# Last two thirds of the modulation: from TensorE row sums to GpSimd products with one-column matmuls

## The chip, the cores and the metric

The kernel runs on one core of one Trainium2 chip. The metric is device time in microseconds (us) of one execution; the median of three runs counts. Times in a profile are those of one profiled execution.

## The reference, cut to what matters

One transformer block over 1024 tokens of width 1024. A condition vector `c` is turned into six vectors of 1024 numbers, the modulation:

```python
c_act = silu(c)
mod = c_act @ w_ada + b_ada            # 1024 x 6144 weights, one row of c
sh1, sc1, g1, sh2, sc2, g2 = split(mod, 6)
h = rmsnorm(x, norm_attn_g) * (1 + sc1) + sh1
proj = h @ w_in                        # q, k, v of two kinds of attention, gate z, b, a
y = concat(dilated_attention(...), gated_deltanet(...)) @ w_out
x = x + g1 * y
h = rmsnorm(x, norm_ffn_g) * (1 + sc2) + sh2
x = x + g2 * ((silu(h @ w_gate) * (h @ w_up)) @ w_down)
return rmsnorm(x, final_norm_g)
```

`sh1` and `sc1` are needed at once. `g1`, `sh2`, `sc2`, `g2` (columns 2048 to 6143 of `w_ada`, the last two thirds) are needed only after the attention, for the first time where the output projection is added to `x`.

## The kernel before, in words

All arithmetic is in fp32. Large matmuls are made of three products of split operands: a weight tile `wr` is loaded, ScalarE rounds it to `wh` (line 215, or 328 for the first projection), and GpSimd writes the remainder `wl = wr - wh` (line 216, or 329). So nearly every projection matmul waits for a product of GpSimd.

The stages, in the order of the program:

1. Small tables, then the first projection (banks `f0` to `f5`, lines 223 to 395): for each of eight slices of `x`, SyncE's queue loads `xt` (line 246) and `wf` (line 249); ScalarE and GpSimd split `wf`; ScalarE scales `x` into `hh` (line 342).
2. `delta(0)` and `delta(1)`, the gated delta rule in two groups of four heads: convolutions, transposes, decay masks `dt` (loaded by line 685, cut to a triangle on GpSimd by line 692), matrices `kk` (line 776), their storing to DRAM in pieces (`lt_d`, line 789), an inverse that is a serial chain on VectorE (lines 862 and 866, begun with the load of `nt` on line 846), and a scan over eight chunks.
3. While those run, TensorE gets filling work from a generator `others()`: gate projections `z0` (eight blocks `g_z0_0` to `g_z0_7`, line 590), then `kd`, `qd`, `vd`, `z1`, `va` and the attention's q and k. Each `z0` block is read out of PSUM by ScalarE (line 611) into one of two buffers `zt`, multiplied by GpSimd (line 612) and stored (line 617); the buffer is free again when the store has landed.
4. Attention, output projection, and the feed-forward part, which fills the second half of the span.

The modulation's last two thirds are a generator as well, `modulation()`. `mixed()` takes one step of it whenever `others()` has handed out more than `MODS` microseconds of filling. There are 64 steps: eight groups `i` of 512 columns, times eight row blocks `k` of 128 rows. A step loads one block `wm` of 128 x 512 (256 KB) into a buffer shared with other tiles (tag `tc`, three buffers), and `rows4` (line 190) multiplies it on TensorE: the condition's column is the stationary operand, 32 columns wide (one of them used), the block is the moving one, in four strips, so that the sums of 512 columns stand on four partitions of a PSUM bank `mods`. After eight steps VectorE transposes the row into columns (`by_columns`).

The order of instructions on every engine and queue is fixed when the program is built. A scheduler takes instructions by priority as soon as their operands and buffers are free in its own account; `urgent()` raises the priority of what stands inside it by 6000 places, and the loads of the `wm` blocks stand inside it. On the chip each engine, and SyncE's one DMA queue, then goes through its list strictly in order and waits where a semaphore isn't there yet.

Of the kernel before, what the change touches and what calls it, by code (L numbers as in the profile page):

```python
# [10 lines left out]
F32 = mybir.dt.float32  # L11
F32R = mybir.dt.float32r
AF = mybir.ActivationFunctionType
ALU = mybir.AluOpType
# [4 lines left out]
P = 128  # L19
T = 1024  # L20
D = 1024
KT = D // P
TB = T // P
HALF = 512
# [1 line left out]
NF = FT // 2  # L26
SKEW = 4
TCB = 3
MODS = 1.9
EARLY = 1  # L30
LEVELS = ("qd", 4), ("z1", 28)
TAIL = 4
# [37 lines left out]
def build(tc, I, out):  # L70
    nc = tc.nc
    es = ExitStack()
    op = es.enter_context

    def pool(name, side="left", bufs=1, space=None):
        st = ExitStack()
        kw = {} if space is None else {"space": space}
        p = st.enter_context(
            tc.tile_pool(name=name, bufs=bufs, side=side, reuse_waits="tile", **kw)
        )  # L80
        return p, st
# [7 lines left out]
    def const(shape, name, dt=F32):  # L89
        return cp.tile(shape, dt, name=name, tag=name)  # L90

    def urgent():
        return tc.high_priority(offset=6000)
# [8 lines left out]
    ones = onesr.bitcast(F32)  # L102
    nc.gpsimd.affine_select(
        out=tri, in_=tri, pattern=[[1, P]], compare_op=ALU.is_ge, fill=0.0,
# [9 lines left out]
    def small(name, shape, src):  # L114
        t = const(shape, name)
        nc.sync.dma_start(t, src)
        return t


    pd, sd = pool("pd")  # L120
    wp, swp = pool("wp", side="right")
    pv, spv = pool("pv", side="right")
# [7 lines left out]
    def psb(name, tag, bufs):  # L130
        return pg.tile([P, HALF], F32, name=name, tag=tag, bufs=bufs)

    def gbank(name):
        return psb(name, "g", 2)
# [4 lines left out]
    def tbank(name):  # L139
        return psb(name, "t", 2)  # L140

    def abank(name):
        return psb(name, "a", 1)

    def ybank(name):
        return psb(name, "y", 1)

    def start(name, tag, shape=None, dt=F32):

        n = {"xp": 2, "qk": 4, "lu": 5, "o": 2, "VN": 2, "R": 1, "tc": TCB, "yt": 1, "os": 1, "zl": 1}.get(tag, 2)  # L150
        return pd.tile(shape or [P, T], dt, name=name, tag=tag, bufs=n)
# [3 lines left out]
    cc = const([P, KT + 31], "cc")  # L155
# [13 lines left out]
    bada = small("bada", [P, 48], I["bada"])  # L169
    ga = small("ga", [P, KT], I["ga"])  # L170
    mod = const([P, 48], "mod")
# [4 lines left out]
    for j in range(3):  # L176
        n = min(HALF, 1152 - HALF * j)
        ps = tbank(f"ps_R{j}")
# [11 lines left out]
    def rows4(ps, win, w, nt, last):  # L190

        v = w.rearrange("p (t j m) -> p j t m", j=4, m=32)
        for j in range(4):
            nc.tensor.matmul(
                ps[32 * j : 32 * j + 32, 0 : 32 * nt], win, v[:, j], start=False, stop=last, skip_group_check=True
            )

    def by_columns(ps, out, nt, add=None, shape=None, tag="os"):  # L200

        t = shape or start("turned", tag, [P, 256])
        nc.vector.transpose(t[:, 0 : 32 * nt], ps[:, 0 : 32 * nt])
        if add is None:
            nc.vector.tensor_copy(out, t[:, 0 : 32 * nt : 32])
        else:
            nc.vector.tensor_tensor(out=out, in0=t[:, 0 : 32 * nt : 32], in1=add, op=ALU.add)
# [116 lines left out]
    for k in range(KT):  # L324
# [6 lines left out]
        if k == 0:  # L331
            for i in range(KT):
# [4 lines left out]
                out=G1[:, 0:1], in0=mod[:, 8:9], scalar=1.0, in1=ga[:, 0:1], op0=ALU.add, op1=ALU.mult  # L337
            )
            scaled(0, 1)
        for hf in range(2):  # L340
# [3 lines left out]
                out=hl[k][:, cs], in0=xts[k][:, cs], scalar=G1[:, k : k + 1], in1=hh[k][:, cs].bitcast(F32),  # L344
                op0=ALU.mult, op1=ALU.subtract,
# [69 lines left out]
    for i in range(2):  # L415
        ps = aux[:, P * i : P * i + P]
# [183 lines left out]
    for q in range(2):  # L600
        ps = gbank(f"g_qd{q}")
# [30 lines left out]
    def v4(t):  # L632
        return t.rearrange("p (g n h) -> p g n h", g=2, n=8)
# [5 lines left out]
    for g in range(2):  # L639
        nc.vector.tensor_tensor(  # L640
            out=v4(t1)[:, g], in0=ba[:, 1, g], in1=dtb[:, 4 * g : 4 * g + 4].unsqueeze(1).to_broadcast([P, 8, 4]), op=ALU.add
# [437 lines left out]


    def modulation():
        pm = ybank("mods")
        for i in range(8):
            t0 = 16 + 4 * i
            ps = pm[:, P * (i % 4) : P * (i % 4 + 1)]
            if i % 4 == 0:
                nc.vector.memset(pm, 0.0)
            for k in range(KT):
                w = pd.tile([P, HALF], F32, name=f"wm_{i}_{k}", tag="tc", bufs=TCB)
                with urgent():  # L1090
                    nc.sync.dma_start(w, I["wada"][k * P : (k + 1) * P, t0 * P : t0 * P + HALF])
                rows4(ps, cc[:, k : k + 32], w, 4, k == KT - 1)
                yield
            t = pv.tile([P, 256], F32, name=f"mt{i}", tag="zt", bufs=2)
            by_columns(ps, mod[:, t0 : t0 + 4], 4, bada[:, t0 : t0 + 4], shape=t)
        nc.vector.scalar_tensor_tensor(
            out=G2, in0=mod[:, 32:40], scalar=1.0, in1=gff, op0=ALU.add, op1=ALU.mult
        )

    done = set()  # L1100
    mods = modulation()

    def others():
# [19 lines left out]
    def mixed():  # L1123

        t = 0.0
        for c in others():
            yield c
            t += c
            if t > MODS and not quiet[0]:
                t = 0.0  # L1130
# [239 lines left out]
    ps = abank("g2t")  # L1370
# [47 lines left out]
    for hf in range(2):  # L1418
# [3 lines left out]
        for d in range(KT):  # L1422
            slabs = [(wsplit(I["wo"][d, 0], 512, f"wo{d}_0_{hf}"), 0)]
            t = x2[d, hf]
            nc.sync.dma_start(t, _.xp[2 * d + hf])
            ps = (gbank, sbank)[d % 2](f"wo{d}_0_{hf}")
            run(gemm(ps, slabs, yh, yl, cs))
            with urgent():
                nc.vector.scalar_tensor_tensor(
                    out=t, in0=ps, scalar=mod[:, 16 + d : 17 + d], in1=t, op0=ALU.mult, op1=ALU.add,  # L1430
# [14 lines left out]
        ps, pb = ybank(f"ssq2_{hf}"), abank(f"rsb2_{hf}")  # L1445
# [3 lines left out]
        with urgent():  # L1449
            for tb in range(4):  # L1450
# [4 lines left out]
                out=dg, in0=ident.unsqueeze(1).to_broadcast([P, 4, P]),  # L1455
                in1=r4.unsqueeze(2).to_broadcast([P, 4, P]), op=ALU.mult,
# [189 lines left out]
    for k in range(4):  # L1646
# [3 lines left out]
        t = px.tile([P, HALF], F32, name=f"t2_{k}", tag="m", bufs=5)  # L1650
# [231 lines left out]
```

## Time and profile before

| | us |
|---|---|
| runs | 1458.61 median of 3 (1457.56 to 1468.36) |
| span of the profiled execution | 1472.9 |
| TensorE busy | 1400.0 (95%) |
| VectorE busy | 872.2 (59%) |
| ScalarE busy | 667.2 (45%) |
| GpSimd busy | 287.0 (19%), 267 instructions |
| DMA | 244.64 MB, mean 166 GB/s |

In the profile PE is TensorE, PEld its weight load, DVE VectorE, ACT ScalarE, POOL GpSimd, SP SyncE, and SPq SyncE's queue of DMA issues. A row of the timeline reads: start, duration, engine, line, operation, output<-inputs with their shapes, count, and in brackets the idle time before it and what ended it. The page has no other time of the profiled execution than its span, which is 14.3 us above the median of the runs.

### The profile page before, as it was taken

Reading aid. Unit: us, or ns where it says so; the run is one execution under the profiler, and the core shown is the slowest. Engines: PE = TensorE matmul, PEld = TensorE weight load, DVE = VectorE, ACT = ScalarE, POOL = GpSimd, SP = SyncE. Lnnn points to the kernel's source line nnn. Section 1 sums busy time; section 2 is a strip of 40 time slices with the busy share of each in tenths; the row PEclk is TensorE's granted clock in tenths of the full one; section 3 lists DMA queues with packets and bytes.
Section 4 is the critical chain, followed back from the end, with each engine's and each line's share of the span. In section 5 each row is a group of like instructions: output and inputs, shape, how many; then the busy total and the mean of one; then the engine's idle time right before and its main releaser. Section 6 shows DMA issues by size and latency. Waiting matters only on the chain.

```text
span 1472.9 us, 24559 instructions
## 1 busy us (share of the span) xinstructions
PE 1400.0 (95%) x8984; PEld 1140.2 (77%) x8984; DVE 872.2 (59%) x1676; ACT 667.2 (45%) x1279; POOL 287.0 (19%) x267
## 2 busy tenths in 40 slices
PE   7998999988999989999999979999999999999997
PEld 4777767877889868777777758888888888888886
DVE  3687843565733332276525896766666676565477
ACT  3488414248122244476526733333333333445446
POOL 1344512244302332544235000000000000000000
PEclk9998999899957999999999989999999999999999
DMA  8736573475511535743165534454444565866666
GB/s 306 247 108 173 151 221 113 134 218 147 170 46 44 154 104 142 203 129 116 51 220 187 158 122 142 164 160 161 152 157 152 158 217 178 277 206 209 196 219 236
DMA packets 171345, 244.64 MB, mean 166 GB/s; under 512 B 33014, under 2 KB 76327, under 8 KB 171224
## 3 DMA queue, kind: packets, MB, share of 16 engines
q1 hardware_dynamic: 171224, 243.07, 52.7%
q8 instruction: 71, 1.16, 0.3%
q14 instruction: 50, 0.41, 0.1%
HBM read 180.25 MB, written 67.48 MB: 168 GB/s over the span
## 4 chain that ended last, share of the span: by engine, by line
PE 62%; DVE 7%; DMA 5%; ACT 2%; issue 2%; POOL 1%; SPq 0%; ACTq 0%; DVEq 0%
PE wga L1513 8%; PE wua L1513 8%; PE X L1699 6%; PE g_a L567 5%; PE wuc L1513 4%; PE wgc L1513 4%; PE Z L1699 4%; PE wo L567 4%; PE y L1293 3%; PE tr L1276 2%; PE Y L1699 2%; PE g_va L590 2%; PE wub L1513 2%; PE wgb L1513 2%; PE S L1252 1%
## 5 line engine op out<-in xcount | busy, mean ns | idle before, releaser
L1503 DVE TENSOR_TENSOR wl_db<-wr_db,wh_db 128x512 fp32r<-128x512 f32 x77 | 53.2, 691 | 76.1 <-ACT wh_db L1502 75.7
L1502 ACT CAST wh_db<-wr_db 128x512 fp32r<-128x512 f32 x77 | 47.9, 622 | 98.3 <-PE X L1699 41.3
L1699 PE MATMUL X<-wl_db,wh_da 128*128 128x512 f32 x176 | 68.6, 390 | 0.1
L1699 PE MATMUL X<-wh_db,wl_da 128*128 128x512 f32 x176 | 68.5, 389 | 0.0
L1699 PE MATMUL X<-wh_db,wh_da 128*128 128x512 f32 x176 | 68.5, 389 | 0.0
L1263 POOL TENSOR_SCALAR X<-X,sc 128x128 f32<-128x128 f32 (+7 forms) x64 | 47.7, 750 | 67.7 <-DVE sc L1262 55.1
L1261 ACT ACTIVATE X<-X,sc 128x128 f32<-128x128 f32 (+7 forms) x64 | 49.5, 775 | 23.8 <-DVE sc L1256 18.1
L1256 DVE CUSTOM_DVE_ANT_0 X<-S,ng 128x512 f32<-128x512 f32 (+3 forms) x64 | 36.8, 586 | 33.8 <-PE S L1253 21.7
L1222 DVE SCALAR_TENSOR_TENSOR QS<-raw,QS 64x1024 fp32r<-64x1024 f32 x8 | 12.6, 1572 | 70.3 <-ACT QS L1221 70.3
L567 PE MATMUL wo<-yh,wh_wo 128*128 128x512 f32 x128 | 52.0, 408 | 2.1 <-DVE xo L1339 1.0
L1503 DVE TENSOR_TENSOR wl_da<-wr_da,wh_da 128x512 fp32r<-128x512 f32 x77 | 52.6, 685 | 1.2 <-ACT wh_da L1502 1.2
L567 PE MATMUL g_a<-hh,wh_a 128*128 128x512 f32 x128 | 50.6, 395 | 0.0
L567 PE MATMUL g_a<-hh,wl_a 128*128 128x512 f32 x128 | 50.5, 395 | 0.0
L567 PE MATMUL wo<-yh,wl_wo 128*128 128x512 f32 x128 | 50.5, 396 | 0.0
L567 PE MATMUL g_a<-hl,wh_a 128*128 128x512 f32 x128 | 50.2, 392 | 0.0
L567 PE MATMUL wo<-yl,wh_wo 128*128 128x512 f32 x128 | 50.2, 394 | 0.0
L1502 ACT CAST wh_da<-wr_da 128x512 fp32r<-128x512 f32 x77 | 47.3, 616 | 5.8 <-PE wua L1513 5.8
L1293 PE MATMUL y<-et,va 128*64 128x128 f32 x576 | 46.0, 280 | 1.8 <-ACT et L1281 1.8
L1502 ACT CAST wh_wg_s<-wg_s 128x512 fp32r<-128x512 f32 x33 | 20.5, 622 | 58.0 <-PE wuc L1513 22.6
L1276 PE MATMUL tr<-ident,X 128*128 128x128 f32 x288 | 44.5, 280 | 2.2 <-ACT et L1281 2.0
L216 POOL TENSOR_TENSOR wl_wo<-wr_wo,wh_wo 128x512 fp32r<-128x512 f32 x24 | 32.8, 1366 | 57.4 <-ACT wh_wo L215 50.7
L1293 PEld LDWEIGHTS y<-et,va 128*64 128x64 f32 x576 | 33.7, 136 | 12.8 <-issue 8.7
(530 smaller groups left out, 4429.8 us busy)
## 6 DMA issues: line engine op xcount, KB each, us to landing
wr_da<-ao_d SPq DMA_DIRECT2D x77, 256.0 KB, 2.9
wm<-in_wada SPq DMA_DIRECT2D x64, 256.0 KB, 3.5
wr_wg<-in_wg SPq DMA_DIRECT2D x48, 256.0 KB, 3.0
wr_wu<-in_wu SPq DMA_DIRECT2D x48, 256.0 KB, 2.7
ao_d<-a SPq DMA_DIRECT2D x44, 256.0 KB, 2.2
wr_wd<-in_wdn SPq DMA_DIRECT2D x44, 256.0 KB, 3.1
wr_db<-wt_d SPq DMA_DIRECT2D x44, 256.0 KB, 2.7
ao_d<-as SPq DMA_DIRECT2D x33, 256.0 KB, 2.0
```

Of the source, the lines that this page charges most:

```text
L216: (eng or nc.gpsimd).tensor_tensor(out=lo[:, :n], in0=raw[:, :n], in1=hi[:, :n].bitcast(F32), op=ALU.subtract)
L567: last[0] = nc.tensor.matmul(ps, a[:, w0], b[k0 + k4][:, cs], start=(i == 0), stop=(i == n - 1))
L590: last[0] = nc.tensor.matmul(ps[:, :n], a[k][:, ts_], b[:, w0], start=(i == 0), stop=(i == 23))
L1256: nc.vector.tensor_tensor_reduce(out=X[:, c0:c1], in0=ps[:, 0 : c1 - c0], in1=ng[:, u + c0 : u + c1], scale=1.0, scalar=(3e38 if m is None ...
L1261: nc.scalar.activation(X[:, 0:nk], X[:, 0:nk], AF.Exp, scale=-1.0, bias=m, accum_out=sc[:, 2:3])
L1263: nc.gpsimd.tensor_scalar(out=X[:, 0:nk], in0=X[:, 0:nk], scalar1=sc[:, 3:4], scalar2=0.0, op0=ALU.mult, op1=ALU.add)
L1276: nc.tensor.transpose(ps[:, (kb - c0) * P : (kb - c0 + 1) * P], X[:, kb * P : kb * P + P], ident)
L1293: nc.tensor.matmul(yps[64 * e : 64 * e + 64, yc], va[:, kb, 64 * e : 64 * e + 64], ets[e][:, kb, :], start=(kb == 0), stop=(kb == qb),)
L1502: nc.scalar.copy(hi, src)
L1503: (eng or nc.vector).tensor_tensor(out=lo, in0=src, in1=hi.bitcast(F32), op=ALU.subtract)
L1513: nc.tensor.matmul(ps, a[:, w0], b, start=(first and k == 0 and n_ == 0), stop=(k == 3 and n_ == 2), skip_group_check=True,)
L1699: nc.tensor.matmul(bank[b], a[:, ts_], w, start=(first and f == 0 and n_ == 0), stop=(f == NF - 1 and n_ == 2), skip_group_check=True,)
```

## The change

A step of `modulation()` no longer uses TensorE. GpSimd multiplies the block by the condition's column (one number for each partition) and adds it to an accumulator `wa` of 128 x 512; the first block of a group writes the accumulator directly. That is 64 products and 56 sums. When a group's eight blocks are summed, four matmuls with the accumulator's 128 x 128 pieces as stationary operand and a single column of ones as the moving one sum the partitions; their results are columns at once, so the transposes go, and one addition of the bias serves all eight groups. The `wm` blocks get five buffers of their own (tag `wm`), the accumulators two, the loads are asked for three steps ahead, and `MODS` rises from 1.9 to 2.5. The room comes from a smaller scratch area for DMA descriptors.

```diff
-MODS = 1.9
+MODS = 2.5
...
     def modulation():
         pm = ybank("mods")
-        for i in range(8):
-            t0 = 16 + 4 * i
-            ps = pm[:, P * (i % 4) : P * (i % 4 + 1)]
-            if i % 4 == 0:
-                nc.vector.memset(pm, 0.0)
-            for k in range(KT):
-                w = pd.tile([P, HALF], F32, name=f"wm_{i}_{k}", tag="tc", bufs=TCB)
-                with urgent():
-                    nc.sync.dma_start(w, I["wada"][k * P : (k + 1) * P, t0 * P : t0 * P + HALF])
-                rows4(ps, cc[:, k : k + 32], w, 4, k == KT - 1)
-                yield
-            t = pv.tile([P, 256], F32, name=f"mt{i}", tag="zt", bufs=2)
-            by_columns(ps, mod[:, t0 : t0 + 4], 4, bada[:, t0 : t0 + 4], shape=t)
+        units = [(i, k) for i in range(8) for k in range(KT)]
+        ws_, accs = {}, {}
+
+        def load(u):
+            i, k = units[u]
+            ws_[u] = pd.tile([P, HALF], F32, name=f"wm_{i}_{k}", tag="wm", bufs=5)
+            with urgent():
+                nc.sync.dma_start(ws_[u], I["wada"][k * P : (k + 1) * P, (16 + 4 * i) * P : (20 + 4 * i) * P])
+
+        def columns(i):
+            for j in range(4):
+                nc.tensor.matmul(
+                    pm[:, 4 * i + j : 4 * i + j + 1], accs[i][:, j * P : (j + 1) * P], ones[:, 0:1], start=True, stop=True
+                )
+
+        for u in range(3):
+            load(u)
+        for u, (i, k) in enumerate(units):
+            if u + 3 < len(units):
+                load(u + 3)
+            w = ws_.pop(u)
+            if k == 0:
+                accs[i] = pd.tile([P, HALF], F32, name=f"wa_{i}", tag="wa", bufs=2)
+            o = accs[i] if k == 0 else w
+            nc.gpsimd.tensor_scalar(
+                out=o, in0=w, scalar1=cc[:, k : k + 1], scalar2=0.0, op0=ALU.mult, op1=ALU.add
+            )
+            if k > 0:
+                nc.gpsimd.tensor_tensor(out=accs[i], in0=accs[i], in1=w, op=ALU.add)
+            if k == 3 and i > 0:
+                columns(i - 1)
+            yield
+        columns(7)
+        nc.vector.tensor_tensor(out=mod[:, 16:48], in0=pm[:, 0:32], in1=bada[:, 16:48], op=ALU.add)
...
-    nc = _bacc.Bacc("TRN2", target_bir_lowering=False, num_devices=1)
+    nc = _bacc.Bacc("TRN2", target_bir_lowering=False, num_devices=1, dynamic_dma_scratch_size=256)
```

The list of instructions that the build makes of this differs from the list before in three places that the prediction uses. Numbers are places in a queue.

```
SyncE queue, after: places 1-5 the first five wm blocks, 6-10 cc and the tables, 11-31 sixteen more wm blocks
                    (up to group 2, block 4) with bada, ga and the three R_d stores, 32 xt0, 33 wf0
             before: places 1-8 wa8, cc, tables, bada, ga; 9 xt0, 10 wf0
GpSimd, after: places 16-50 the first 20 products and 14 sums, 53 wl_f0;  80-83 the four dt selects of delta(0);
               84-178 the other 44 products and 42 sums, with kt0, kt1, qd0, qd1, zt0_2, U0_0, tt0, zt0_3 among them;
               179 zt0_4, 180 zt0_5, 181 zt0_6, 182 wl_kd2_1
TensorE, after: row 525 columns of groups 0 and 1 (behind g_z0_3), then kk; 583 g_z0_4; 611 columns of group 2, 613 of 3,
                619 of 4, 621 of 5, 623 of 6; 625 g_z0_5, 649 g_z0_6, 673 g_z0_7; 697 g_kd2_0
```

## The prediction

> **What bounds the kernel now.** I read the page first, then TensorE's waits, then the modulation's matmuls by stage, and last the timeline of the start and of the stage in which the modulation runs.
>
> ```profile
> PE 1400.0 (95%) x8984; PEld 1140.2 (77%) x8984; DVE 872.2 (59%) x1676; ACT 667.2 (45%) x1279; POOL 287.0 (19%) x267
> PE   7998999988999989999999979999999999999997
> POOL 1344512244302332544235000000000000000000
> PE 62%; DVE 7%; DMA 5%; ACT 2%; issue 2%; POOL 1%; SPq 0%; ACTq 0%; DVEq 0%
> ```
>
> TensorE is the bound: busy 95%, and no slice but the first, one in the middle and the last is under 80%. GpSimd has much room on average (19%), but all of it is spent in the first 22 slices (810 us), and there it makes the operands that TensorE waits for. So the change takes work from the bound and gives it to an engine with room; what decides is when GpSimd does it. In the profiled execution the span is 1472.9 us, 14.3 above the runs' median of 1458.61; I make the sum as a difference and add it to the median. A measurement of this kernel can tell about 1% (15 us) from no change.
>
> **What TensorE gets back.** The old matmuls by stage (window, then PE busy and instructions), the price of one step among other matmuls, and the waits that they carried:
>
> ```profile
> 165.00:240.00 75.00, 10.80 (x200) 3.98 (x200) 1.43 (x4) 0.98 0.66 197
> 240.00:400.00 160.00, 16.68 (x240) 6.01 (x240) 0.92 (x3) 0.95 0.52 155
> 178.04 0.39 PE L567 MATMUL g_kd<-hl,wh_kd 128*128 128x512 f32 x1
> 178.27 0.39 PE L567 MATMUL g_kd<-hh,wl_kd 128*128 128x512 f32 x1
> 178.59 0.42 PE L196 MATMUL mods<-wm,cc 128*32 128x128 f32 x8
> 178.94 0.50 PE L567 MATMUL g_kd<-hh,wh_kd 128*128 128x512 f32 x1
> 179.28 0.39 PE L567 MATMUL g_kd<-hl,wh_kd 128*128 128x512 f32 x1
> PE mods L196 <- DVE mt L203: 4.3, 2, 3.9
> PE mods L196 <- DMA wm<-in_wada: 4.7, 3, 1.8
> ```
>
> A matmul follows another after 0.23 us (178.04 to 178.27). Around a step it takes 0.67 from 178.27 to 178.94 and 0.34 to 179.28, 1.01 for what would take 0.46: a step of eight records costs 0.55. After 165 us there are 440 records, 55 steps, one of them before the first `kd` matmul at 167.29 (shown below): 54 x 0.55 = 29.7, and one wait of 3.9, together 33.6. The ten steps before 167 I count below, with the stall that swallows them.
>
> The new columns, four matmuls a group, have a near row:
>
> ```profile
> L1451 PEld LDWEIGHTS ssq<-onesr,acc x16: 186/192/192, 787.2 to 817.8; 128*128 128x128 f32 x16
> ```
>
> This is the same form (sum of partitions by a column of ones), 16 records for 8 matmuls, each bound by a weight load of 0.192. A group's four matmuls cost 8 x 0.192 = 1.5 us. All groups but the last stand before the `kd` matmuls, where TensorE will be waiting anyway; the last costs its 1.5. Net 32.1 to gain. The stage is 95% TensorE, but chains of VectorE and ScalarE run beneath it, which the old steps covered in part; I take 80% of it, -26, and keep 0 and -33.6 as bounds.
>
> **What a step costs on GpSimd.** The same forms, fp32, 128 x 512, and what else stands in its queue there:
>
> ```profile
> L1263 POOL TENSOR_SCALAR X<-X,sc 128x512 f32<-128x512 f32 x8 | 5.5, 695 | 9.2 <-DVE sc L1262 7.2 <-PE S L1253 1.2 <-PE tr L1276 0.8
> L1441 POOL TENSOR_TENSOR acc<-acc,sq 128x512 f32<-128x512 f32 x10 | 13.7, 1368 | 9.7 <-ACT sq L1440 9.4
> L1441 POOL TENSOR_TENSOR acc<-acc,sq x10: 1285/1300/1657, 771.0 to 812.7; 128x512 f32<-128x512 f32 x10
> L801 POOL TENSOR_TENSOR kt<-kt,kds 128x1024 f32<-128x1024 f32 x4 | 7.6, 1914 | 9.6 <-ACT kt L722 6.1 <-DVE kds L755 3.5
> L816 POOL TENSOR_TENSOR qd<-qd,eb 128x1024 f32<-128x1024 f32 x4 | 9.5, 2386 | 6.9 <-ACT eb L815 5.3 <-DMA zg_d<-zt 1.6
> L612 POOL TENSOR_TENSOR zt<-zt,ngh 128x256 f32<-128x256 f32 x16 | 14.2, 887 | 38.9 <-ACT zt L611 32.3 <-DMA lt_d<-dt 6.5
> wm<-in_wada SPq DMA_DIRECT2D x64, 256.0 KB, 3.5
> zg_d<-zt SPq DMA_DIRECT2D x16, 128.0 KB, 2.3
> ```
>
> A product 0.695, a sum 1.368 in the mean: 2.06 us a step, 64 x 0.695 + 56 x 1.368 = 121 us in all. Bounds by the sum's least and greatest duration: 1.98 and 2.35. A block takes 3.5 from issue to landing; with five buffers four other steps, 8.2 us, lie between the freeing of a buffer and the use of its next block, so the loads hide. Without that cover each step would be 3.5 longer.
>
> The Trainium skill (GPSIMD Engine Reference, section 4.1, Engine selection) speaks against the change: elementwise sums belong on VectorE, GpSimd is about half as fast with two inputs. Its section 3.1 gives some 2.6 cycles an element for such a sum; at its 1.2 GHz, 512 elements make 1.11 us as an estimate from that page. With that in place of 1.368 the result below would be some 13 us less; the measured row decides.
>
> **The start.** The row blocks are loaded with raised priority, and with five buffers of their own nothing holds them back; so in the written order 21 of them stand ahead of `xt0` in SyncE's queue (place 32), and 34 products and sums ahead of `wl_f0` in GpSimd's. The queue waits at each block for a buffer that GpSimd must free.
>
> ```profile
> 1.40 0.33 SPq L157 DMA_DIRECT2D cc<-in_cc  x1
> 4.39 0.43 SPq L246 DMA_DIRECT2D xt<-in_xT  x1
> 8.94 2.36 SPq L184 DMA_DIRECT2D R_d<-Rs  x3
> 3.86 1.28 ACT L158 ACT_TABLE_LOAD   x1 [3.86 <-DMA cc<-in_cc]
> 5.15 0.21 ACT L158 ACTIVATE cc<-cc 128x8 f32<-128x8 f32 x1
> 11.58 1.27 POOL L329 TENSOR_TENSOR wl_f<-wf,wh_f 128x512 fp32r<-128x512 f32 x1 [9.12 <-ACT wh_f L328]
> 12.18 0.79 PE L236 MATMUL f<-hh,wh_f 128*128 128x512 f32 x1 [0.36 <-ACT hh L342]
> 12.91 0.80 PE L236 MATMUL f<-hh,wl_f 128*128 128x512 f32 x1
> ```
>
> GpSimd can begin when `cc` is through the silu: 5.4 us before; five block issues of 0.4 now stand ahead of it, and their 1.25 MB, so about 8.0. The block before `xt0` needs the buffer of block 16: 16 products and 14 sums, 11.1 + 19.2, and a memset of 0.3, 30.6 us, to 38.6. Its issue and two `R_d` stores take some 1.6: `xt0` is issued at 40.2 instead of 4.39, 35.8 later. Before, the first matmul came 7.8 after that issue and the remainder 8.5, with `wa8` and the stores in between; with those done ahead I take 2.5 off: **+33**. TensorE has nothing else to do: all that follows needs `x`.
>
> **The stall in the middle.** GpSimd's next steps, places 84 to 178, come in one run behind the last `dt` select, and TensorE's own list has the columns of groups 2 to 6 between `g_z0_4` and `g_z0_5`: it stops there until GpSimd has summed group 6.
>
> ```profile
> 131.91 1.09 POOL L692 TENSOR_SCALAR_AFFINE_SELECT dt<-dt 128x1024 f32<-128x1024 f32 x1 [1.36 <-DMA dt<-G_d]
> 164.59 0.28 PE L590 MATMUL g_z<-wh_z,hh 128*128 128x256 f32 x1
> 164.71 0.28 PE L590 MATMUL g_z<-wh_z,hl 128*128 128x256 f32 x1
> 167.17 0.28 PE L590 MATMUL g_z<-wl_z,hh 128*128 128x256 f32 x1
> 167.29 0.40 PE L567 MATMUL g_kd<-hh,wh_kd 128*128 128x512 f32 x1
> ```
>
> The selects end at 133.0, with the start's +33 at 166.0. Up to place 165 follow 39 products and 37 sums, 27.1 + 50.6, two `kt`, two `qd` and a `zt`, 3.8 + 4.8 + 0.9: 87.2, to 253.2. That place frees the buffer of the last block, and in SyncE's queue the store of `zt0_1` stands behind that block's load. `zt` has two buffers, so ScalarE can't read out `g_z0_3` before this store lands, and `g_z0_5` needs its bank: three issues 1.1, landing 2.3, read-out 0.4, to 257.0. Blocks 5 to 7 of `z0` are 72 matmuls at 0.12, 8.7; `g_z0_7` waits besides for `zt0_3` (place 176: 5 products, 4 sums, a memset and itself, 10.9, to 264.1), its store and a read-out, to 267.2, and ends 2.9 later. The first `kd` matmul comes at 270.1 instead of 167.3: 102.8 later, of which the start has 33: **+70**. The steps saved before 167 lie inside this. VectorE's inverse is held as long (its load of `nt` stands behind the last block too), so nothing of it can be done in the meantime.
>
> **Sum.** +33 + 70 - 26 = +77; 1472.9 + 77 = 1550 for an execution like the profiled one, **1535** against the median of the runs.
>
> The rows give 53 steps on the path (15 at the start, 38 in the middle): at 1.98 and 2.35 us the sum moves by -4 and +15. The gain's bounds move it by +26 and -8. `cc`, the head of the middle run and the restart of loads I can place to some 10 us either way. Least 1535 - 22 = 1513, most 1535 + 51 = 1586; both ends together are unlikely upwards, and a clock granted more freely after the pauses (0.95 to 0.98 in the two windows above) could take some 10 more off. I give 1503 to 1573.
>
> **Rivals.** (1) GpSimd's work is hidden, as the change reads in the source: steps spread through the filling, TensorE freed. Then 64 x 0.55 + the waits 9.0 - 64 x 0.192 for the columns = -32, 1427 us. For it speaks GpSimd's 19%; against it, that each queue goes through its list in order, and the lists have the runs ahead of `wl_f0` and `wl_kd2_1`. This is the case on the other side: with u for a step, the change costs 53u - 32, from the terms above; it is no slower only if u is under 0.60 us, less than the product alone (0.695). Chance 0.03, and 0.03 for an end within 1%.
>
> (2) VectorE and GpSimd hinder each other in the `kk` part, where both work: sums at 1.66 and products in proportion at 0.84, 2.5 a step, +23, and the gain half lost, +13: 1571. Against it: VectorE is idle for most of both runs, since it waits for the same things. Chance 0.12.
>
> (3) The blocks come too slowly, because SyncE's queue holds other transfers between them (`lt_d` pieces that wait for VectorE): a share of 10 of the 38 middle steps bare, 10 x 3.5 = +35, 1570. Chance 0.07.
>
> **How the numbers follow.** The forecast has 0.75, rivals 1 to 3 0.06, 0.12 and 0.07. Faster by over 1% is half of rival 1, 0.03; within 1% the other half, 0.03; slower 0.94. The range is the forecast's own; the greater part of rivals 2 and 3 lies in it or at its edge.
>
> **What would show each step.** Right: the first `f` matmul at some 45 us instead of 12.18, behind 31 steps on GpSimd; products near 0.70 and sums near 1.37; TensorE idle for about 60 us before the columns and the `zt` read-out, with the first `kd` matmul near 270; and from there to the end some 26 less than before. Wrong: `xt0` issued early; GpSimd's steps scattered among the remainders; a TensorE without a pause between `g_z0_4` and `g_z0_5`; or steps of a clearly other duration. If the pauses are there and the total isn't, the stretch after `kd` has to be shorter by more than the removed matmuls.

## The result, and the profile after

The changed kernel takes 1549.43 us (median of 4 runs, 1539.89 to 1561.48), the kernel before 1461.21 (4 runs beside it): ratio 1.0599, 95% interval 1.0548 to 1.065, so 88 us slower. The forecast was 1535 in a range of 1503 to 1573. Here and below, a ratio leaves out executions over 1.5% above the fastest of their kernel and is not the quotient of the two medians.

The profiled execution after has a span of 1539.0 us, 66.1 over that of before (1472.9). The 66 of the profiles and the 88 of the medians fit together: the execution profiled before ran 13.4 us over its kernel's median (span and the 1.7 us that the runs have beside a span), the one profiled after ran 8.8 under its own, and 66.1 + 13.4 + 8.8 = 88.3. Why runs of one kernel differ so much stands in the last section.

The page after: busy times, and the tenths of 40 slices for TensorE, GpSimd and the granted clock.

```profile
PE 1367.0 (89%) x8536; PEld 1130.7 (73%) x8536; DVE 879.6 (57%) x1659; ACT 667.2 (43%) x1279; POOL 406.6 (26%) x387
...
PE   1799632889989998999999979999999999999997
...
POOL 7324899323541233254434300000000000000000
PEclk9999855989999998999999999999999999999999
```

TensorE is busy 33 us less in a longer span. That is no count of the removed work: with the same 8536 matmuls it is busy 1407.3 us in e3 below, at a mean granted clock of 0.930 instead of 0.950. It has lost two places: the first slice (1) and slices 5 to 7 (6, 3, 2), and in the same slices GpSimd is at its busiest (7; 8, 9, 9).

The start, from the timeline (start, duration, engine and line, in brackets the idle time before and what ended it):

```profile
0.80 2.29 SPq L1091 DMA_DIRECT2D wm<-in_wada  x5
9.85 0.69 POOL L1108 TENSOR_SCALAR wa<-wm,cc 128x512 f32<-128x512 f32 x1 [7.39 <-DMA rb<-in_rel]
39.60 0.36 SPq L246 DMA_DIRECT2D xt<-in_xT  x1
45.57 0.79 PE L236 MATMUL f<-hh,wh_f 128*128 128x512 f32 x1 [30.55 <-ACT wh_f L328]
```

`xt0` is issued at 39.60 instead of 4.39, because the queue waits for buffers that GpSimd frees, and the first `f` matmul runs at 45.57 instead of 12.18.

GpSimd's steps by group (busy, mean ns of one, idle before):

```profile
L1112 POOL TENSOR_TENSOR wa<-wa,wm 128x512 f32<-128x512 f32 x56 | 75.5, 1348 | 2.0
L1108 POOL TENSOR_SCALAR wm<-wm,cc 128x512 f32<-128x512 f32 x56 | 38.7, 696 | 1.3 <-DMA wm<-in_wada 0.8 <-PE trv L833 0.5
```

A product costs 0.696 and a sum 1.348 here. GpSimd waited for blocks 0.8 us in all: the loads are hidden.

The middle, from the timeline:

```profile
166.67 1.09 POOL L692 TENSOR_SCALAR_AFFINE_SELECT dt<-dt 128x1024 f32<-128x1024 f32 x1 [1.14 <-DVE vd L532]
246.23 12.04 SPq L1091 DMA_DIRECT2D wm<-in_wada  x8
253.28 1.87 PE L1095 MATMUL mods<-onesr,wa 128*128 128x1 f32 x8 [12.41 <-POOL wa L1112]
258.80 0.92 SPq L617 DMA_DIRECT2D zg_d<-zt  x2
261.45 0.89 ACT L611 ACTIVATE zt<-g_z 128x256 f32<-128x256 f32 x2 [46.27 <-DMA zg_d<-zt]
261.89 0.58 PE L590 MATMUL g_z<-wh_z,hh 128*128 128x256 f32 x1 [6.74 <-ACT zt L611]
264.69 1.34 DVE L851 TENSOR_TENSOR nt<-nt,bpr 128x1024 f32<-128x1024 f32 x1 [46.75 <-DMA nt<-lt_d]
273.95 0.40 PE L567 MATMUL g_kd<-hh,wh_kd 128*128 128x512 f32 x1
```

Behind the last select GpSimd sums one group after another. The last block loads leave SyncE's queue at 258.3, the `zt` store behind them at 258.8. ScalarE has waited 46.27 us for that store, VectorE 46.75 us for the `nt` load behind it, and TensorE 12.4 us for the last of its column groups in this place. One run of steps on GpSimd holds up SyncE's queue and three other engines; the first `kd` matmul comes at 273.95 instead of 167.29.

From there on the changed kernel wins time back: 40.6 us to the end. Where, is shown by windows with like borders (from the first `kd` matmul to the end of the second group's `kk`, and from there to the end of its scan): us, PE busy, PEld, DVE, ACT, POOL, granted clock, DMA share, GB/s. Before:

```profile
167.30:352.40 185.10, 171.00 (x1566) 131.42 (x1565) 103.83 (x234) 72.31 (x161) 51.33 (x50) 0.95 0.58 175
352.40:491.10 138.70, 131.96 (x1274) 120.33 (x1272) 73.16 (x187) 40.57 (x91) 40.91 (x42) 0.80 0.32 90
```

After:

```profile
274.00:448.60 174.60, 156.16 (x1326) 133.59 (x1326) 98.86 (x211) 74.68 (x168) 58.62 (x55) 0.95 0.45 130
448.60:567.40 118.80, 110.27 (x1133) 100.55 (x1133) 76.89 (x184) 38.84 (x91) 39.57 (x37) 0.96 0.29 83
```

The windows don't hold quite the same work. Of the removed steps, 304 records stood in the first stage before, 128 in the second and none behind it: 54 steps, 27 us of TensorE's busy time. But after, the first stage holds 64 matmuls of the filling `g_z` more, the second 65 of them fewer and 56 of `g_a` more, and the rest of the kernel 56 of `g_a` fewer; so the rest is 10.2 us shorter without a step removed there. Only the 40.6 as a whole can be divided. Part of it is the removed work, most plainly in the first stage, which is 10.5 us shorter at the same clock although it holds more filling. Part is the clock: in the second stage, 19.9 us shorter, the execution before ran at 0.80 and the one after at 0.96; 138.7 x 0.80 is 111, 118.8 x 0.96 is 114, so the clock alone could make that difference. How much each gave is not separated by these windows.

### The profile page after: what moved, and what is told of

Its sections match the earlier page's. It is cut to its first block, busy times and chain, and to the rows that moved or that the text cites. A ratio compares the mean times of both kernels' runs of the same rounds, so it can differ in the third digit from the quotient of the medians.

```text
span 1539.0 us, 23746 instructions
## 1 busy us (share of the span) xinstructions
PE 1367.0 (89%) x8536; PEld 1130.7 (73%) x8536; DVE 879.6 (57%) x1659; ACT 667.2 (43%) x1279; POOL 406.6 (26%) x387
## 4 chain that ended last, share of the span: by engine, by line
PE 53%; DVE 5%; DMA 2%; ACT 1%; issue 1%; POOL 0%; SPq 0%; ACTq 0%; DVEq 0%; POOLq 0%
PE wga L1535 8%; PE wua L1535 7%; PE X L1721 6%; PE wo L567 4%; PE wuc L1535 4%; PE wgc L1535 4%; PE Z L1721 4%; PE g_a L567 4%; PE y L1315 3%; PE tr L1298 2%; PE Y L1721 2%; PE wub L1535 2%; PE wgb L1535 2%; PE S L1274 1%; PE S L1275 1%
## 5 line engine op out<-in xcount | busy, mean ns | idle before, releaser
L1112 POOL TENSOR_TENSOR wa<-wa,wm 128x512 f32<-128x512 f32 x56 | 75.5, 1348 | 2.0
L1721 PE MATMUL X<-wl_db,wh_da 128*128 128x512 f32 x176 | 68.6, 390 | 0.2 <-DVE wl_db L1525 0.2
L1721 PE MATMUL X<-wh_db,wh_da 128*128 128x512 f32 x176 | 68.6, 390 | 0.0
L236 PE MATMUL f<-hh,wh_f 128*128 128x512 f32 x48 | 21.0, 437 | 30.6 <-ACT wh_f L328 30.6
L590 PE MATMUL g_z<-wh_z,hh 128*128 128x256 f32 x128 | 40.1, 314 | 7.1 <-ACT zt L611 7.1
```

What stands on the lines that cost most here:

```text
L590: last[0] = nc.tensor.matmul(ps[:, :n], a[k][:, ts_], b[:, w0], start=(i == 0), stop=(i == 23))
L1112: nc.gpsimd.tensor_tensor(out=accs[i], in0=accs[i], in1=w, op=ALU.add)
L1721: nc.tensor.matmul(bank[b], a[:, ts_], w, start=(first and f == 0 and n_ == 0), stop=(f == NF - 1 and n_ == 2), skip_group_check=True,)
```

## The experiments

All ratios are to the kernel before in runs beside it on the same chip; its median there was 1466 to 1473 us. e10 ran on another chip than the rest.

**e1_plain: the loads without raised priority.**

```diff
-            with urgent():
-                nc.sync.dma_start(ws_[u], ...)
+            nc.sync.dma_start(ws_[u], ...)
```

> The block loads are issued without raised priority; everything else is the changed kernel. In the queues the first blocks then stand behind the loads of the first stage, and of GpSimd's products and sums 15 stand ahead of wl_vd0_1 and wl_vd1_1, 19 ahead of wl_qd0_1, 28 between the dt selects and qd1, the rest scattered up to wl_a4_0_1. Theory (runs of steps ahead of what TensorE waits for, brought there by the raised loads): the start's 33 us vanish (first f matmul near 12 us); what is left of the runs costs some 10 us at wl_vd and 15 to 20 at the zt buffers, the removed matmuls give some 30 back: about 1455 us, 1440 to 1475. Rival (the steps cost what they cost on GpSimd wherever they stand, by sharing something with the other engines): still over 1530.

Measured: 1514.24 us, ratio 1.0294 (1.0191 to 1.0398). The start is as expected, and the run behind the selects is cut short; the total is not as expected.

```profile
11.99 0.79 PE L236 MATMUL f<-hh,wh_f 128*128 128x512 f32 x1 [0.36 <-ACT hh L342]
200.40 0.50 PE L567 MATMUL g_kd<-hh,wh_kd 128*128 128x512 f32 x1 [0.42 <-ACT zt L611]
```

The raised priority makes the start's 33 us; the first `kd` matmul is still 33 us late (200.40 for 167.29). But of the 73 us won there over the changed kernel (273.95), the end keeps 26.9 (span 1512.1), or 45 by the ratios. Something else costs time once the steps stand among other work.

**e2_middle_freed: the first 21 loads raised, the rest tied behind the weight loads and remainders of the filling.** The ordering edges (`spl` is the last weight load, `pll` the last remainder that the program has issued; the product gets the same edge on `pll`):

```diff
+            if u < 21: (as before)
+            else:
+                with tc.issue_after(spl[0].ins):
+                    nc.sync.dma_start(ws_[u], ...)
...
-            if k == 3 and i > 0:
+            if k == 7 and i > 0:
                 columns(i - 1)
```

> The first 21 block loads stay raised, as in the changed kernel; the other 43 are tied behind the weight load and their products behind the remainder (wl) that precede them in the program, and a group's columns come four steps later. So the run ahead of wl_f0 stays whole and the run behind the dt selects shrinks from 86 products and sums to 5. Theory: the start's +33 stays (first f matmul near 45.6 us), the middle's +70 goes (first kd matmul near 200 instead of 274), and the removed matmuls still give 26 to 40: 1454 to 1470 us against some 1461 before. Rival 1 (one stall only moves into the other: TensorE catches up or loses the same elsewhere): 1500 or more. Rival 2 (VectorE and GpSimd hinder each other): steps later in the program lengthen to 1.66 a sum and the total stays over 1490.

Measured: 1533.45 us, ratio 1.0436 (1.0344 to 1.0528).

```profile
45.22 0.80 PE L240 MATMUL f<-hh,wh_f 128*128 128x512 f32 x1 [30.59 <-ACT wh_f L332]
205.30 0.40 PE L571 MATMUL g_kd<-hh,wh_kd 128*128 128x512 f32 x1
```

Start and middle are separate, as foreseen: the start's stall stays (45.22), the middle's is gone (205.30 is 38 late, of which the start has 33). Yet the total is 60 us over before: of the 69 us won in the middle, the end keeps 8 (span 1530.9 against 1539.0), or 24 by the ratios; the others were given back later. Sums stayed at 1.366 us, so the steps themselves did not lengthen.

**e3_spread: all loads and products tied in this way, none before the end of `z0`, one step for each 1.9 us of filling.**

```diff
-MODS = 2.5
+MODS = 1.9
...
-            if t > MODS and not quiet[0]:
+            if t > MODS and not quiet[0] and "z0" in done:
```

> All block loads and products are tied in the same way, none begins before the z0 filling is through, one step for each 1.9 us of filling as in the kernel before, and a group's columns come four steps later. GpSimd's products and sums stand in short runs (at most 14) between the remainders from wl_kd3 on. Theory (only the place of the steps costs): both stalls are gone and the removed matmuls give 26 to 40, so 1421 to 1436 us, faster than before by 2 to 2.7%. Rival 1 (a run of ten steps, 10 us, ahead of a remainder still stops TensorE, some 64 x 1.0 us in all): 1470 to 1500. Rival 2 (the removed matmuls were hidden under VectorE's and ScalarE's chains): no gain, 1455 to 1465.

Measured: 1535.01 us, ratio 1.0452 (1.0357 to 1.0547). Neither stall is there, and it is 62 us slower than before. My theory, that only the place in the queues costs, falls. The two lines of VectorE's inverse, before and then in this version:

```profile
L866 DVE TENSOR_TENSOR tt<-tt,tm 128x31 f32<-128x31 f32 (+15 forms) x62 | 27.2, 439 | 2.0
L862 DVE TENSOR_TENSOR tm<-nt,tt 128x31 f32<-128x31 f32 (+15 forms) x62 | 26.1, 421 | 2.2
```

```profile
L866 DVE TENSOR_TENSOR tm<-nt,tt 128x31 f32<-128x31 f32 (+15 forms) x62 | 49.0, 790 | 2.2
L870 DVE TENSOR_TENSOR tt<-tt,tm 128x31 f32<-128x31 f32 (+15 forms) x62 | 46.7, 753 | 2.1
```

The serial chain takes 95.7 us instead of 53.3. How, shows the timeline, one form of it before (first fence) and beside GpSimd's steps in this version:

```profile
173.81 0.32 DVE L862 TENSOR_TENSOR tm<-nt,tt 128x156 f32<-128x156 f32 x1
```

```profile
186.26 0.69 DVE L866 TENSOR_TENSOR tm<-nt,tt 128x156 f32<-128x156 f32 x1
186.99 1.29 DVE L870 TENSOR_TENSOR tt<-tt,tm 128x156 f32<-128x156 f32 x1
...
186.05 0.74 POOL L1113 TENSOR_SCALAR wm<-wm,cc 128x512 f32<-128x512 f32 x1
186.76 2.71 POOL L1117 TENSOR_TENSOR wa<-wa,wm 128x512 f32<-128x512 f32 x2
```

An operation of 0.32 us takes 0.69 beside a product and 1.29 beside a sum: VectorE gets through one operation for each of GpSimd's. The new theory: the two engines keep each other out for whole operations. The Trainium skill (SBUF — State Buffer, Who interferes with whom) has this as a rule: a VectorE instruction with two SBUF inputs contends with a GpSimd instruction that reads SBUF, not with one that only writes it.

**e4_thin_sums: the changed kernel with sums over 16 of 512 columns.** The run of steps in the queues stays.

```diff
-                nc.gpsimd.tensor_tensor(out=accs[i], in0=accs[i], in1=w, op=ALU.add)
+                nc.gpsimd.tensor_tensor(out=accs[i][:, 0:16], in0=accs[i][:, 0:16], in1=w[:, 0:16], op=ALU.add)
```

> The changed kernel with its 56 sums cut to the first 16 of 512 columns (the other columns' sums are left out); products, loads and columns stay, and the two runs stand at nearly the same places. A step costs some 0.8 us of GpSimd instead of 2.06. Theory (53 steps on the path at the step's GpSimd time): 53 x 1.26 = 67 less, some 1482 us, first f matmul near 27 us. Rival (the blocks' arrival then sets the pace, 1.3 us or more for each 256 KB): 35 to 40 less, some 1512 us. If GpSimd's time is not what the runs cost: still over 1540.

Measured: 1493.2 us, ratio 1.0129 (1.0009 to 1.0248).

```profile
32.13 0.79 PE L236 MATMUL f<-hh,wh_f 128*128 128x512 f32 x1 [17.97 <-ACT wh_f L328]
227.46 0.40 PE L567 MATMUL g_kd<-hh,wh_kd 128*128 128x512 f32 x1
```

```profile
L1108 POOL TENSOR_SCALAR wm<-wm,cc 128x512 f32<-128x512 f32 x56 | 40.0, 717 | 5.6 <-DMA wm<-in_wada 5.0 <-DMA lt_d<-dt 0.4
L1112 POOL TENSOR_TENSOR wa<-wa,wm 128x16 f32<-128x16 f32 x56 | 14.6, 261 | 3.9
```

A short sum still costs 0.261, so a step falls by some 1.09 us, not 1.26; 53 x 1.09 = 58. The first `kd` matmul is 46.5 earlier, the span 40.6 shorter, the median 56 lower (69 by the ratios to the kernel before). So the time of GpSimd's steps on the path is what the two stalls are made of. The start is 13.4 us earlier, not 18; GpSimd now waits 5.0 us for blocks instead of 0.8, so the arrival of the blocks takes a part, without setting the pace.

**e5_tensor_thin: the kernel before, with seven of eight steps cut on TensorE.**

```diff
-                rows4(ps, cc[:, k : k + 32], w, 4, k == KT - 1)
+                if k == KT - 1:
+                    rows4(ps, cc[:, k : k + 32], w, 4, True)
+                else:
+                    nc.tensor.matmul(ps[0:32, 0:32], cc[:, k : k + 32], w[:, 0:32], start=False, stop=False, ...)
```

> The kernel before, with seven of eight steps of each modulation group cut on TensorE from eight records (four strips of 128 columns) to one matmul of 32 columns; loads, buffers and VectorE's transposes stay, GpSimd gets nothing (the sums of the cut columns are left out). It prices the removed matmuls alone. As the prediction sized them (80% of 32 us): ratio to before 0.982, some 26 us less. If they only filled waits for VectorE's chains: 0 to 8 us less. If the 40 us that the changed kernel won back between the first kd matmul and the output projection are theirs alone: 38 or more less.

Measured: 1449.74 us, ratio 0.9875 (0.9806 to 0.9944), some 18 us less (8 to 28). The forecast's share lies in the interval, 38 and nothing don't. The runs of both kernels at clocks from 0.976 to 0.979 are 1449.48 and 1450.0 against 1456.69 and 1460.52, 7 to 11 us apart. The profile has 336 records fewer (8648 for 8984), since a step of one small matmul still makes two of them; the change has 448 fewer. In that proportion, as an estimate from these runs, removing the matmuls could have brought 24 us, or 9 to 15 at like clocks, in the best case.

**e6_spread_memsets: the spread version with GpSimd writing only.**

```diff
-                nc.gpsimd.tensor_scalar(out=o, in0=w, scalar1=cc[:, k : k + 1], ...)
+                nc.gpsimd.memset(w, 0.0)
+            nc.gpsimd.memset(w[:, 0:256], 0.0)
...                       (for k == 0 one more memset, of the accumulator)
-                nc.gpsimd.tensor_tensor(out=accs[i], in0=accs[i], in1=w, op=ALU.add)
+                for _r in range(3):
+                    nc.gpsimd.memset(w, 0.0)
```

> The spread version with each product replaced by two memsets of the loaded block (512 and 256 columns) and each sum by three memsets of 512 columns: GpSimd is busy at the same places for some 2 us a step, but reads nothing (products and sums are left out). In the spread version VectorE's inverse, a serial chain of 62 products and 62 sums, took 95.7 us in all instead of 53.3, one VectorE operation for each GpSimd operation that ran beside it. Theory (a GpSimd operation with two inputs or one from SBUF and a VectorE operation with two such inputs keep each other out for a whole operation): the inverse is back at 53 to 56 us, VectorE busy near 875 instead of 920, and the total 40 to 60 below the spread version: 1475 to 1495 us or less. Rival (GpSimd's queue order, remainders and memsets behind the steps, costs the time): the inverse is short, but the total stays within 15 us of the spread version's 1535. Rival (any GpSimd work slows VectorE): the inverse stays over 85 us.

Measured: 1493.91 us, ratio 1.0179 (1.0116 to 1.0242), 41 us under the spread version. GpSimd is as busy (413.0 us in all against 409.5), and the inverse is short again:

```profile
L870 DVE TENSOR_TENSOR tt<-tt,tm 128x31 f32<-128x31 f32 (+15 forms) x62 | 26.7, 431 | 2.1
L866 DVE TENSOR_TENSOR tm<-nt,tt 128x31 f32<-128x31 f32 (+15 forms) x62 | 26.7, 430 | 3.4 <-POOL tt L861 1.3
```

53.4 us instead of 95.7, and the total moves by the same amount. The new theory holds, and the Trainium skill's rule with it: memsets leave VectorE alone. It explains only a part of the losses elsewhere: in e1 and e2 the inverse takes 68.6 and 70.4 us, 15 and 17 more than before, where the totals are some 41 and 60 us over. What remains here, 44 us over e5, is another thing. The timeline and 4 us windows (TensorE busy and records, clock, DMA share, GB/s) show one of its places:

```profile
240.94 1.33 PE L927 MATMUL lw<-tc,dt 64*64 64x64 f32 x10 [4.76 <-ACT tc L919]
```

```profile
232.00:236.00 4.00, 4.00 (x121) 1.00 0.56 144
236.00:240.00 4.00, 0.17 (x1) 0.76 0.81 264
240.00:244.00 4.00, 3.06 (x19) 0.50 0.98 294
244.00:248.00 4.00, 4.00 (x25) 0.50 0.69 227
...
280.00:284.00 4.00, 4.00 (x19) 0.50 0.64 228
284.00:288.00 4.00, 4.00 (x26) 0.77 0.34 137
```

```profile
237.86 0.37 ACT L1071 COPY sp_vd<-g_vd 128x256 f32<-128x256 f32 x1 [6.53 <-DMA pj_d<-sp_qd]
240.13 0.37 ACT L1071 COPY sp_vd<-g_vd 128x256 f32<-128x256 f32 x1 [1.89 <-DMA pj_d<-sp_qd]
240.52 0.36 ACT L919 COPY tc<-lv 32x256 f32<-32x256 f32 x1
```

ScalarE's copy `tc` stands in its queue behind two read-outs `sp_vd`, and these wait for stores of `sp_qd`. In SyncE's queue these stores stand among block loads and weight loads, which wait for buffers that GpSimd frees (5.4 and 4.3 us of waiting between 224 and 242 us). TensorE pauses 4.76 us, and then works at half clock for more than 40 us, without a further pause.

**e7_placed: the spread version without steps in the inverses.**

```diff
+            rate = 99.0
+            if "va0" in done: rate = 1.2
+            elif "qd" in done and "z1" not in done: rate = 1.2
-            if t > MODS and not quiet[0] and "z0" in done:
+            if t > rate and not quiet[0]:
```

> The spread version with its steps kept out of the two inverses: none before the vd filling, one for each 1.2 us of filling in vd and z1, none in va0, and one for each 1.2 us from va1 on. Theory (the inverses are what the steps lengthen): the inverse stays under 62 us in all, and the total is 1450 to 1480 us, near the kernel before. Rival (GpSimd's own queue, with runs up to 24 steps ahead of the memsets that the scan's matmuls need): lv and st late by 20 or more in the second scan, total 1490 to 1520.

Measured: 1505.15 us, ratio 1.0281 (1.0202 to 1.036), 30 under the spread version. The inverse still takes 67.0 us, 14 more than before: the first, with no step beside it, takes 28.8 us, but steps still reach GpSimd while the second runs, which takes 38.3 (before: 27.6 and 25.6). So the placement was missed in part; the total lies in the rival's range (the last `lv` 25 us late, the last `st` 22).

**e8_vector and e9_gpsimd_same_places: the same places, the steps once on VectorE and once on GpSimd.**

```diff
+            elif "qd" in done and "vd" not in done: rate = 0.6
...
-            (product and sum on GpSimd)
+            with tc.issue_after(inv[0].ins):      # e8 only: the inverse's last operation
+                nc.vector.scalar_tensor_tensor(
+                    out=accs[i], in0=w, scalar=cc[:, k : k + 1], in1=accs[i], op0=ALU.mult, op1=ALU.add
+                )
```

> The steps on VectorE instead of GpSimd: one instruction a step (block times the condition's column, plus the accumulator), 128x512, priced at 0.75 to 0.95 us by VectorE's rows of that kind; half of them in the vd filling behind the first inverse, the other half from va1 on behind the second, none inside an inverse. Some 55 us of VectorE, put where it is idle most; GpSimd gets nothing, TensorE only the columns. Theory (what the change loses is where and on which engine the steps stand, and the removed matmuls are worth some 20 us): inverse at 53 to 56 us, total 1445 to 1470, at or a little under the kernel before on the same chip. Rival (TensorE falls into pauses without its own modulation steps as filling, and runs at half clock after each): 1475 to 1500 in spite of a short inverse.

> The same places in the program as the version with the steps on VectorE, but the steps on GpSimd as in the changed kernel (a product and a sum). Theory (GpSimd's operations keep VectorE's two-input operations out, and its memsets and remainders for the scans stand behind the steps in its queue): 20 to 40 us over the version on VectorE, 1475 to 1505. Rival (place alone decides): within 10 us of the version on VectorE.

Measured: on VectorE 1462.66 us, ratio 0.9986 (0.9947 to 1.0026); on GpSimd 1525.36, ratio 1.0386 (1.0325 to 1.0448). So the two lie 63 us apart, but not by the engine alone: only e8 ties the steps behind the inverse, and in e9 steps run beside the second one, which takes 40.5 us (the first 27.5). e9's inverse takes 68.1 us in all, e8's 54.3, so 14 of the 63 are the inverse's; the longest waits of TensorE that e9 has more of are for `tn` (14.7 us for 4.4) and for ScalarE's `tc` (12.3). On VectorE a step is one instruction of 0.788 us:

```profile
L1119 DVE SCALAR_TENSOR_TENSOR wa<-wm,cc,wa 128x512 f32<-128x512 f32 x56 | 44.0, 788 | 6.3 <-DMA wm<-in_wada 5.2
```

```profile
PE trq_0False L718 <- ACT qd L540: 7.8, 1, 7.8
```

The total is that of the kernel before, so nothing is gained; whether VectorE's 44 us cost nothing, or just what the removed matmuls bring, it doesn't tell. In the midst of `z0` TensorE now waits 7.8 us for ScalarE's `qd` (the second line above), and from 125 to 170 us its granted clock (the number after the busy times) is lower; before, and then on VectorE:

```profile
125.00:170.00 45.00, 41.20 (x363) 36.84 (x363) 35.08 (x47) 31.06 (x60) 25.61 (x19) 0.89 0.56 151
```

```profile
125.00:170.00 45.00, 36.86 (x265) 33.86 (x264) 28.79 (x40) 31.09 (x59) 19.34 (x12) 0.73 0.32 78
```

That the removed matmuls had kept TensorE busy through this wait is my reading; e10 tries it.

**e10_mixed_engines: as e8, with the first group of eight steps left on TensorE inside `z0`.**

> The version with the steps on VectorE, but its first group of eight steps stays on TensorE, inside the z0 filling, as in the kernel before; the other 56 steps stand on VectorE as in that version. In the version with all steps on VectorE, TensorE waited 7.8 us for a transposed qd behind z0 and ran at a granted clock of 0.73 from 125 to 170 us. Theory (those steps were the filling that kept TensorE from pausing there): the wait falls under 3 us, the clock of 125 to 170 is 0.9 or more, the first kd matmul is back at 167 to 169 instead of 172.9, and the total is 5 to 15 us under the version on VectorE: 1447 to 1458, ratio to before 0.985 to 0.995. Rival (the pause only moves on): total within 4 us of the version on VectorE, ratio 0.995 to 1.002.

Measured: 1466.31 us, ratio 0.9975 (0.9934 to 1.0017): the rival. In the profiled execution (1480.65 us, the longest of the twelve) the 7.8 us wait is gone, but two waits for blocks, 1.3 and 2.3 us, stand in its place, the clock from 125 to 170 us is 0.77 and not 0.9, and the first `kd` matmul comes at 174.4. So the pause has only moved, and the reading that those eight steps were the missing filling is not borne out. What the record does show is that the gain of e8 goes with a lower clock: its twelve runs have a median clock of 0.956, the sixteen of the kernel before beside them 0.968, and at like clocks e8 is 15 us faster (1458.03 us at 0.966 against 1472.85 at 0.967). Why the clock is lower stays open. No version that I ran beats the kernel before by more than can be measured, except e5, which leaves work out.

## Why the prediction was right, and where its sizes were off

- *The start, +33.* Right: 33.4 by the first `f` matmul, `xt0` at 39.60 for 40.2. GpSimd began at 9.85 for 8.0 and its sums were a little faster. e1 and e2 show that the hoisted loads make it, e4 that GpSimd's time does.
- *The middle, +70.* Right: 73.3. The chain was the one described: the last block load, the `zt` store behind it, ScalarE's read-out, TensorE; read-out at 261.45, first matmul behind it at 261.89 for 257.0, first `kd` at 273.95 for 270.1. e2 removes it alone. TensorE's wait for the columns ends first, at 253.28, and the one for the store's read-out last, at 261.89; no run takes away one of them alone.
- *The price of a step.* 0.696 and 1.348 for 0.695 and 1.368. The 1.11 us for a sum that I estimated from the Trainium skill (GPSIMD Engine Reference, 3.1) are not met: the least duration here is 1.25. So the 13 us less by that estimate did not come.
- *The gain, -26.* The profiles give back 40.6, which is more than the term's bound of 33.6, but a part of it is the clock of the second scan in the execution before. If the two stalls are as long in every run as in the profile (33.4 and 73.3), the medians' 88 leave 18.5 for the gain. e5 measures 18 us with clocks as they fell, 7 to 11 at like clocks, for 336 of the change's net 448 records. So the term lies within its bounds and was, if anything, sized too high. Its direct pricing (so many steps times 0.55, 80% of it at the end) can't be checked more closely, since TensorE's busy time follows the clock too.
- *The sum.* +77 against +66 in the profiles and +88 in the medians. Put on the median it gave 1535; two of the four runs are within 6 us of it (1539.89 and 1540.66, clocks 0.952 and 0.950), two are at 1558 and 1561 (0.939 and 0.937). The prediction had no term for a clock that differs from run to run; that the forecast came this close to the two faster runs is in part luck.
- *Rival 2* (VectorE and GpSimd hinder each other) has the right mechanism and the wrong place. In the changed kernel it costs little, just because the run of steps has stalled VectorE too: it waits 46.75 us for `nt`, its inverse begins at 268.9 when all but one sum are done, and takes 56.2 us. Where the middle's stall is removed or cut short, the inverse takes 14 to 17 us more (e1, e2, e7, e9) and 42 in e3. *Rival 3* is out: 0.8 us of waiting for blocks.
- *Rival 1's point* was wrong in its reasoning. It said that the change pays if a step costs under 0.60 us on the path. e3, e7 and e9 have neither of the two runs on that path (first `kd` matmul at 174.1 to 174.4 for 167.29) and are 2.8 to 4.5% slower than before. There is a second price, and the prediction's law 53u - 32 knows nothing of it. One part of it is shown, the longer inverse; the rest, among it stores and loads held up in SyncE's queue as in e6 and a lower clock, is not taken apart by any run.

## What to carry to other kernels

An engine with 19% busy time is free only where nobody needs it: look at what stands behind the new work in its own queue, and at which two-input operations of VectorE run at the same time, above all if they form a serial chain. A load with raised priority and buffers of its own runs ahead until its buffers are full, and takes the work that frees them along; tie such loads to the work that they belong to. And before matmuls are removed from a busy TensorE, remove them alone and see what is gained: here, in e5, TensorE's busy time fell by 26 us and the end came 7 to 18 us earlier.

## What I had not expected of the hardware

- GpSimd's operations that read SBUF and VectorE's with two SBUF inputs exclude each other for whole operations: 0.32 us became 0.69 or 1.29, 53.3 us of chain became 95.7. GpSimd operations that only write (0.525 us memsets, just as dense) left it at 53.4.
- A pause of TensorE of about 4.8 us was followed by more than 40 us at a granted clock of 0.50, though TensorE was busy in every 4 us window of it. The Trainium skill (TensorE: Matmul & The Clock Gate, Part 1) lets the clock fall after an idle window of some 3.4 us and rise again after one busy window of that length; the trace agrees with neither. The clock fell at 238.1, some 2 us into the pause, and rose at 285.9, 45 us after its end; in e8 it fell at 132.2, 2.4 us into the pause of 7.8, and rose at 156.1, some 18 us after its end. What counts as activity there is open: the stage mixes 37 matmuls of 128 x 512 with 336 small ones (64 x 64 and 32 x 32), and e5 goes through the same stage at 1.00.
- With the same instructions a kernel's time follows its clock: the kernel before 1455.84 us at 0.976 and 1480.75 at 0.957, the changed one 1539.89 at 0.952 and 1561.48 at 0.937. Time times clock is 1421 and 1417, and 1466 and 1463. So the 20 us between runs of one kernel go with the clock, and medians of few runs are to be compared with that in mind. The same product is 1418 to 1426 in e1, 1417 to 1421 in e7 and 1414 to 1425 in e9, no more than the 1415 to 1432 of the kernel before in all sessions: what these versions lose goes with clocks of 0.925 to 0.95. That pauses set the clock back is seen at single places (e6, e8); that they make these differences between runs and versions is not shown.
